# Two queue steps between the levels of a gated recurrence, and a weight request moved ahead of two row loads, in a fused decoder layer

## The chip, the cores and the metric

The kernel runs on 1 core of one Trainium2 chip, as one program. The metric is device time in microseconds of one execution. The kernel before took 1952.87 us (median of 3 runs, 1950.09 to 1953.01).

## The reference

One layer of a hybrid decoder for 1024 prompt tokens and 8x8 sample tokens, which share all weights. With D_MODEL 1024 and D_FF 2816, all in f32:

```python
x = x + 0.5 * rms_norm(swiglu(rms_norm(x, norm_ffn1_pre[l]), ffn1_w_gu[l], ffn1_w_down[l]), norm_ffn1_post[l])
h = rms_norm(x, norm_mix_pre[l])
z = h @ w_in[l] + b_in[l]
q, k, v, hq, hf, hi, hg = jnp.split(z, [...], axis=-1)
a, k_new, v_new = attend(q, k, v, attn_sinks[l])        # window of 128, 8 heads over 2 kv heads, a sink per head
a = rms_norm(a, attn_out_norm[l])
f = lb + (1.0 - lb) * jax.nn.sigmoid(hf)                # 4 heads of 128 keys and 128 values
o, S = hgrn2_chunked(silu(hq), 1.0 - f, jnp.log(f), hi, s0)
o = rms_norm(o, hg_out_norm[l]) * jax.nn.silu(hg)
mix = jnp.concatenate([a, o], axis=-1) @ w_out[l]
x = x + rms_norm(mix, norm_mix_post[l])
x = x + 0.5 * rms_norm(swiglu(rms_norm(x, norm_ffn2_pre[l]), ffn2_w_gu[l], ffn2_w_down[l]), norm_ffn2_post[l])
```

Within a chunk the recurrence needs, for query t and key s at or before it, the sum over key channels of q_t, k_s and the product of all gates f between s and t.

## The kernel before, in words

**Columns and precision.** The tokens stand as columns in three groups of 320 (256 prompt tokens and the 64 sample tokens), 384 and 384 (WIDTH). An f32 operand is split in a high and a low part of a faster format: `split` casts the high part on ScalarE (line 222) and subtracts it on VectorE for the low part (line 223). A product is then three matmuls, lines 245 to 247; the third is the one that takes the weights' low part. Weights come through `raw` tiles by SyncE's DMAs.

**The start.** `pre_first` makes the first two products of group 0 from data that it loads in an order of its own. Then it requests the high and low halves of the first unit's other weights (`wts.fill(1)`), loads the rows of x by tokens for the norm (line 635, three tiles: two of 128 rows, one of the 64 sample rows), squares and sums each on ScalarE (`squares`, line 642), and requests the second unit's up weights (`wts.fill(2)`). With the three sums come the root, three diagonal tiles (line 656) and a matmul that spreads the root over all partitions (line 661), copied by line 662. Gates multiply by it (line 698), go through Silu (line 699) and are multiplied by the up product (line 702).

**The feed-forward network of groups 1 and 2** is done by a scheme of seven products per pair of column halves, products 1, 6, 2, 5, 3, 7 and 4 of the down projection, one after another by `pair`. Each takes weights (lines 951 and 954, tiles `raw`, split into `w`) and stored activations (line 966: `ar<-fa`, a tile `ar` of 384 KB, split into a tile `h`). Of these requests one stands ahead in products 5, 3, 7 and 4 (`Ahead` with 1). A bank of four in `mm` is emptied by `put` (lines 979 to 995): an addition on VectorE, or a copy on ScalarE.

**The recurrence** of a group is `intra`, a generator. K (keys), Q (queries) and D (gate products) are kept for 384 columns. First the diagonal (tile `ld`), then levels h = 1, 2, 4, ..., 64: at each, small matmuls of 32x32 (line 1267, bank `lv`) or hxh (line 1307, banks `l32`, `l64`) join keys of the first half of each block of 2h with queries of the second half. VectorE takes the right cells over (line 1297) and multiplies the second halves of Q by gate products (line 1316), GpSimd the first halves of K (line 1318). The next level's matmuls need both. After each level stands a `yield`.

**What sets the order.** The attention and the recurrence of a group are put in two queues, "at" and "hg", by `ready` with a count of the steps of each generator. After each piece of a large product `tick` calls `pace`, which adds to each queue's account the steps left over the ticks left until the group is due (`DUE`: 132, 208, 256); when the two accounts hold 2, or one holds 1.5, both queues go one step on. So the recurrence of group 0 runs beside products 5 and 3 and those that follow, and the steps of "at" come at the same moments. Within that, the framework fixes each engine's instruction order when the program is built: each engine works down one list.

Of the kernel before, what the change touches and what calls it, by code (L numbers as in the profile page):

```python
# [27 lines left out]
NPB = [2, 3, 3]  # L28
# [16 lines left out]
def tile_step(ctx: ExitStack, tc: tile.TileContext, A: dict, O: dict):  # L45
# [10 lines left out]
    def uid(s):  # L56
        cnt[0] += 1
        return f"{s}_{cnt[0]}"
# [4 lines left out]
    def axbank(s="ax"):  # L63
        return ps.tile([P, 512], F32, tag="ax", bufs=4, name=uid(s))
# [5 lines left out]
    def big(dt=F32, shape=(P, 4, 384)):  # L70
        return pp.tile(list(shape), dt, tag="big", bufs=10, name=uid("big"))
# [197 lines left out]
    def rows_of(n, i):  # L269
        return min(P, WIDTH[n] - i * P)  # L270

    def new_h(n):
        return [[hslot(n), hslot(n)], [hslot(n), hslot(n)]]
# [271 lines left out]
    def pre_first(wgu, h, wts):  # L545
# [6 lines left out]
        def queued(eng):  # L552
            return tc.issue_after(last[eng]) if eng in last else nullcontext()

        def do(eng, make):
            with queued(eng):
                last[eng] = make().ins
# [71 lines left out]
        sm = small()  # L629
        V.memset(sm[:, 0], 1.0)  # L630
        rows = []
        for i in range(3):
            r = rows_of(0, i)
            t = big(F32, (P, D))
            nc.sync.dma_start(t[:r], A["x_prompt"][0, i * P:(i + 1) * P] if i < 2 else
                              A["x_sample"].rearrange("b t d -> (b t) d"))
            rows.append(t)

        def squares(i):
            r = rows_of(0, i)  # L640
            t = rows[i][:r]
            do("ACT", lambda: S.activation(t, t, AF.Square, scale=RMS, accum_out=sm[:r, 0, i:i + 1]))

        squares(0)
        squares(1)
        with queued("ACT"), queued("DVE"):
            wts.fill(2)
        last["ACT"], last["DVE"] = formed[1].ins, formed[0].ins
        squares(2)
        do("ACT", lambda: S.activation(junk[:, :P], ones, AF.Silu))  # L650
        do("DVE", lambda: V.tensor_scalar(ms0[:, 0:3], sm[:, 0, 0:3], EPS, None, op0=ALU.add))
        root(sm[:, 1, 0:3], ms0[:, 0:3])
# [390 lines left out]
    def mixing(tp, h):  # L1043
# [206 lines left out]
        def intra(n):  # L1250

            z, w, wp = Z[n], WIDTH[n], P * NPB[n]
            f, Q = z["f"][:, :, :w], z["hq"][:, :, :w]
            K = tp.tile([P, 4, 384], F32, tag="K", name=uid("K"))[:, :, :w]
            D = tp.tile([P, 1524], F32, tag="D", name=uid("D"))
            C = tp.tile([P, 3, 4, 32], F32, tag="cm", name=uid("cm"))
            parts = [(slice(0, P), slice(0, NPB[n]))] + ([(slice(0, NS), slice(2, 3))] if n == 0 else [])

            def span(h):
                return w if h <= 4 else wp  # L1260

            def blocks(s, x, y, h):
                b4 = axbank(s)[:, :384].rearrange("p (j a t) -> p j a t", j=3, a=4)
                for a in range(4):
                    for i in range(span(h) // 32):
                        j, cs, ps_ = i // 4, slice(32 * i, 32 * i + 32), slice(32 * (i % 4), 32 * (i % 4) + 32)
                        PE.matmul(b4[ps_, j, a], x[:, a, cs], y[:, a, cs], start=True, stop=True)  # L1267
                return b4

            def flat(t, rs, js):  # L1270
                return t[rs, js].rearrange("p j a t -> p (j a) t")

            S.activation(K, f, AF.Copy, bias=1.0, scale=-1.0)
            Ds, off, h = [f], 0, 1
            while h <= 64:
                nx = span(h) // (2 * h)
                Dv = Ds[-1][:, :, :2 * nx].rearrange("p a (x e) -> p a x e", e=2)
                Ds.append(D[:, off:off + 4 * nx].rearrange("p (a x) -> p a x", a=4))
                G.tensor_tensor(Ds[-1], Dv[:, :, :, 0], Dv[:, :, :, 1], op=ALU.mult)
                off += 4 * nx  # L1280
                h *= 2
            b4 = blocks("ld", K, Q, 1)
            for rs, js in parts:
                c = flat(C, rs, js)
                V.tensor_tensor(c, flat(b4, rs, js),
                                ident32[rs].unsqueeze(1).to_broadcast([c.shape[0], c.shape[1], 32]), op=ALU.mult)
            V.tensor_tensor(Q, Q, f, op=ALU.mult)
            yield
            At = z["f"]
            h = 1  # L1290
            while h <= 64:
                ws = span(h)
                if h <= 16:
                    b4 = blocks("lv", K, Q, h)
                    for rs, js in parts[:2 if h <= 4 else 1]:
                        c = flat(C, rs, js)
                        V.copy_predicated(c, lmask[h][rs].unsqueeze(1).to_broadcast([c.shape[0], c.shape[1], 32]),
                                          flat(b4, rs, js))
                else:
                    for j0 in range(0, NPB[n], 64 // h + 1):  # L1300
                        js = range(j0, min(NPB[n], j0 + 64 // h + 1))
                        b4 = axbank(f"l{h}")[:, :len(js) * 4 * h].rearrange("p (j a t) -> p j a t", j=len(js), a=4)
                        for j in js:
                            for a in range(4):
                                for c in range(0, P, 2 * h):
                                    k0 = j * P + c
                                    PE.matmul(b4[c:c + h, j - j0, a], K[:, a, k0:k0 + h], Q[:, a, k0 + h:k0 + 2 * h],
                                              start=True, stop=True)
                        Av = At[:, :, P * j0:P * j0 + P * len(js)].rearrange("p a (j t) -> p j a t", j=len(js))
                        for c in range(0, P, 2 * h):  # L1310
                            for j in range(len(js)):
                                S.copy(Av[c:c + h, j, :, c + h:c + 2 * h], b4[c:c + h, j])
                nx = ws // (2 * h)
                Qv, Kv = [t[:, :, :ws].rearrange("p a (x u) -> p a x u", u=2 * h) for t in (Q, K)]
                Dv = Ds.pop(0)[:, :, :2 * nx].rearrange("p a (x e) -> p a x e", e=2)
                V.tensor_tensor(Qv[:, :, :, h:], Qv[:, :, :, h:], Dv[:, :, :, 0:1].to_broadcast([P, 4, nx, h]),
                                op=ALU.mult)
                G.tensor_tensor(Kv[:, :, :, :h], Kv[:, :, :, :h], Dv[:, :, :, 1:2].to_broadcast([P, 4, nx, h]),
                                op=ALU.mult)
                if h == 1:  # L1320
                    G.memset(At[:, :, :w], 0.0)
                if h == 4 and n == 0:
                    z["Ds"] = Ds[0]
                if h == 16:
                    for i in range(4):
                        r, nj = slice(32 * i, 32 * i + 32), 3 if n == 0 and i < 2 else NPB[n]
                        Av = At[r, :, :384].rearrange("p a (j t) -> p j a t", j=3)
                        for j in range(nj):
                            G.tensor_copy(Av[:, j, :, r], C[r, j])
                h *= 2  # L1330
                yield
            z["K"], z["D"] = K, Ds[0]

        def finish_hgrn(n, bank, r, c0):
# [171 lines left out]
        def kv_out(n):  # L1506
            kx, vn = KX[n], VN[n]
            if n == 0:
                nc.sync.dma_start(O["ksT"], kx[:, P + 256:P + 256 + NS])
                for b in range(8):  # L1510
                    nc.sync.dma_start(O["vs"][0, b, 120:128].rearrange("j g d -> j (g d)"), vn[8 * b:8 * b + 8, 3])
            else:
                nc.sync.dma_start(O["kp"], kx[:, P + 256:P + 256 + P])
                nc.sync.dma_start(O["vp"], vn[:, 3])
            yield

        def ready(kind, n):
            if n not in MT:
                MT[n] = new_h(n)
            if kind == "at":  # L1520
                gens = [(attn_block(n, b), 9) for b in range(NPB[n])]
                if n == 0:
                    gens += [(sample_attn(), 11), (kv_out(0), 1)]
                if n == 2:
                    gens.append((kv_out(2), 1))
            else:
                gens = [(intra(n), 8)] + [(hgrn_block(n, b), 3) for b in range(NPB[n])]
                if n == 0:
                    gens.append((sample_hgrn(), 14))
                if n == 2:  # L1530
                    gens.append((state_out(), 1))
            queues[kind] += [[n, g, left] for g, left in gens]
# [50 lines left out]
    h = {}  # L1583
# [231 lines left out]
```

## Time and profile before

| | |
|---|---|
| Runs | 1952.87, 1953.01, 1950.09 us |
| The profiled execution | 1954.31 us |
| Its span, first to last instruction | 1952.6 us |
| TensorE matmuls busy | 1937.5 us (99%) |
| VectorE, ScalarE, GpSimd busy | 1349.6, 929.0, 211.1 us |
| Mean granted TensorE clock | 0.998 |
| Moved by DMA | 362.65 MB, 186 GB/s |

A row of a timeline reads: start in us from the start of the span, us, engine, line, operation, output tile <- input tiles, sizes, count; in brackets the idle time of the engine ahead of it and what ended it. PE is TensorE's matmuls, DVE VectorE, ACT ScalarE, POOL GpSimd, SP SyncE, which issues most DMAs. A row of a table of waits reads: engine, tile, line <- what it waited for: us in total, times, the longest. A row of a table of windows has, for each stretch: its length, the busy time of PE, of its weight loads, of DVE, ACT and POOL with their counts, the granted clock, the share of the DMA engines' time, and GB/s. A row of the chain of waits has: start, us, and the work or the DMA that the end hung on. The line numbers are those of the kernel before; in the kernel after they are 3 higher from the rest of `pre_first` on, and 5 higher behind `intra`.

### The profile page before, as it was taken

The page shows a single profiled execution, that of the slowest core. Times are in us where ns is not written, and L with a number is a line of the kernel's source. Part 1 is how long each engine was busy: PE and PEld are TensorE (multiplying, and loading weights), DVE is VectorE, ACT ScalarE, POOL GpSimd, SP SyncE. Part 2 cuts the span into 40 slices and gives each one's busy share as a digit, 9 for nine tenths or more (in the row PEclk, how much of TensorE's full clock was granted, in tenths as well). Part 3 has the DMA queues.
Part 4 walks back from the last instruction along what each step waited for, and adds up shares of the span by engine and source line. Part 5 has one row for each costly group of instructions (what it writes and reads, how often), then busy time and mean ns, then how long its engine had stood idle before and what let it go on. Part 6 is the DMA issues. An engine that isn't in the chain of part 4 may idle for free.

```text
span 1952.6 us, 34158 instructions
## 1 busy us (share of the span) xinstructions
PE 1937.5 (99%) x13451; PEld 1825.4 (93%) x13451; DVE 1349.6 (69%) x2188; ACT 929.0 (48%) x1637; POOL 211.1 (11%) x213
## 2 busy tenths in 40 slices
PE   9999999999999999999999999999999999999998
PEld 9999999999998987788899898999999999999887
DVE  5876667776558666875667765745987877655666
ACT  6633333444445544654345455745544444444453
POOL 0000000000004112111232431101000000000202
PEclk9999999999999999999999999999999999999999
DMA  9643345556677555675434333556555645577974
GB/s 322 209 143 129 144 162 186 179 183 208 236 236 228 163 146 163 213 228 153 120 101 141 115 112 117 190 166 206 174 204 187 217 177 186 206 237 232 308 260 141
DMA packets 162492, 362.65 MB, mean 186 GB/s; under 512 B 16524, under 2 KB 60236, under 8 KB 162316
## 3 DMA queue, kind: packets, MB, share of 16 engines
q1 hardware_dynamic: 161324, 358.65, 55.5%
q8 instruction: 105, 1.72, 0.4%
q10 hardware_dynamic: 1008, 1.84, 0.3%
q14 instruction: 55, 0.45, 0.1%
HBM read 283.78 MB, written 77.63 MB: 185 GB/s over the span
## 4 chain that ended last, share of the span: by engine, by line
PE 94%; DMA 2%; DVE 2%; ACT 1%; issue 1%; POOL 0%; SPq 0%; DVEq 0%; POOLq 0%; ACTq 0%
PE mm L245 28%; PE mm L247 28%; PE mm L246 28%; PE c L247 1%; PE c L245 1%; PE c L246 1%; DMA ar<-fa 1%; PE pv L1234 1%; PE sc L1193 1%; PE pT L1219 1%; PE lv L1267 0%; DMA raw<-in_ffn_w_gu_dram 0%; DMA x1N<-big 0%; PE av L1368 0%; DMA big<-in_x0T_dram 0%
## 5 line engine op out<-in xcount | busy, mean ns | idle before, releaser
L245 PE MATMUL mm<-h,wsph 128*128 128x320 f32 (+1 forms) x1280 | 409.5, 320 | 0.2 <-DVE sg L702 0.2
L247 PE MATMUL mm<-h,wspl 128*128 128x320 f32 (+1 forms) x1280 | 403.5, 317 | 1.2 <-DVE wspl L223 1.2
L246 PE MATMUL mm<-h,wsph 128*128 128x320 f32 (+1 forms) x1280 | 404.4, 316 | 0.0
L223 DVE TENSOR_TENSOR wspl<-raw,wsph 128x1024 fp32r<-128x1024 f32 x200 | 250.0, 1251 | 156.4 <-ACT wsph L222 156.0
L222 ACT CAST wsph<-raw 128x1024 fp32r<-128x1024 f32 x200 | 209.3, 1048 | 270.6 <-PE mm L246 205.4
L222 ACT CAST w<-raw 128x512 fp32r<-128x512 f32 (+1 forms) x226 | 169.3, 754 | 240.3 <-PE mm L246 119.8
L223 DVE TENSOR_TENSOR w<-raw,w 128x512 fp32r<-128x512 f32 (+1 forms) x226 | 196.6, 874 | 87.8 <-ACT w L222 87.3
L245 PEld LDWEIGHTS mm<-h,wsph 128*128 128x128 f32 x1280 | 240.4, 188 | 5.4 <-issue 3.2
L247 PEld LDWEIGHTS mm<-h,wspl 128*128 128x128 f32 x1280 | 239.9, 188 | 3.0 <-DVE wspl L223 1.7
L246 PEld LDWEIGHTS mm<-h,wsph 128*128 128x128 f32 x1280 | 240.5, 188 | 1.5 <-issue 0.7
L245 PE MATMUL mm<-h,w 128*128 128x384 f32 x704 | 235.6, 335 | 0.0
L246 PE MATMUL mm<-h,w 128*128 128x384 f32 x704 | 235.6, 335 | 0.0
L247 PE MATMUL mm<-h,w 128*128 128x384 f32 x704 | 230.5, 335 | 0.0
L245 PE MATMUL mm<-w,h 128*128 128x512 f32 x462 | 182.2, 398 | 1.9 <-DVE big L979 1.0
L246 PE MATMUL mm<-w,h 128*128 128x512 f32 x462 | 181.0, 392 | 0.0
L247 PE MATMUL mm<-w,h 128*128 128x512 f32 x462 | 178.9, 392 | 0.0
L216 POOL TENSOR_TENSOR sm<-sm,mhalf 128x3 f32<-128x3 f32 (+4 forms) x37 | 33.7, 913 | 1187.6 <-DVE sm L304 462.3
L245 PEld LDWEIGHTS mm<-h,w 128*128 128x128 f32 x704 | 132.2, 188 | 0.2 <-ACT big L793 0.2
L222 ACT CAST w<-t 128x512 fp32r<-128x512 f32 x176 | 107.3, 621 | 52.4 <-PE mm L247 46.9
L246 PEld LDWEIGHTS mm<-h,w 128*128 128x128 f32 x704 | 132.1, 188 | 0.0
L247 PEld LDWEIGHTS mm<-h,w 128*128 128x128 f32 x704 | 131.7, 188 | 0.0
L223 DVE TENSOR_TENSOR w<-t,w 128x512 fp32r<-128x512 f32 x176 | 119.0, 687 | 10.5 <-ACT w L222 10.3
(348 smaller groups left out, 3688.5 us busy)
## 6 DMA issues: line engine op xcount, KB each, us to landing
raw<-in_ffn_w_gu_dram SPq DMA_DIRECT2D x154, 512.0 KB
raw<-in_ffn_w_down_dram SPq DMA_DIRECT2D x74, 512.0 KB
raw<-in_w_in_dram SPq DMA_DIRECT2D x54, 512.0 KB
ar<-fa SPq DMA_DIRECT2D x70, 384.0 KB
big<-in_ffn_w_down_dram SPq DMA_DIRECT2D x88, 256.0 KB
fb<-big SPq DMA_DIRECT2D x44, 512.0 KB
raw<-fb SPq DMA_DIRECT2D x40, 512.0 KB
fa<-big SPq DMA_DIRECT2D x22, 768.0 KB
```

What stands on the lines that cost most here:

```text
L216: G.tensor_tensor(y, x, mhalf[:y.shape[0], :y.shape[1]], op=ALU.pow)
L222: formed[1] = S.copy(hi, src)
L223: return (lo_eng or V).tensor_tensor(lo, src, hi.bitcast(F32), op=ALU.subtract)
L245: PE.matmul(out, a[0], b[0], start=first, stop=False, skip_group_check=resume)
L246: PE.matmul(out, a[0], b[1], start=False, stop=False, skip_group_check=resume)
L247: r = latest[0] = PE.matmul(out, a[1], b[0], start=False, stop=last, skip_group_check=resume)
L1193: PE.matmul(banks[g][:, i * 256:i * 256 + wk], zq[64 * g:64 * g + 64, 2 * pr + i, b * P:(b + 1) * P], kx[64 * g:64 * g + 64, k0:k0 + wk], ...
L1219: PE.transpose(bank[:, (i * nk + kb) * P:(i * nk + kb + 1) * P], pt[g][:, i, kb * P:(kb + 1) * P], ident)
L1234: PE.matmul(ob[q0:q0 + 64, c:c + 64], pT[g][:, k1:k1 + 64], vn[:, vb, g * 64:g * 64 + 64], start=kb == 0, stop=kb == nk - 1)
```

## The change

There are two edits. `intra` gives way twice, not once, after each of the levels 1 to 32, and `ready` counts 14 steps for it, not 8. `pre_first` loads row tile 0, squares it, requests the second unit's up weights, and then loads and squares the row tiles 1 and 2.

```diff
-        for i in range(3):
+
+        def load_rows(i):
             r = rows_of(0, i)
             t = big(F32, (P, D))
             nc.sync.dma_start(t[:r], A["x_prompt"][0, i * P:(i + 1) * P] if i < 2 else
...
+        load_rows(0)
         squares(0)
-        squares(1)
         with queued("ACT"), queued("DVE"):
             wts.fill(2)
         last["ACT"], last["DVE"] = formed[1].ins, formed[0].ins
-        squares(2)
+        for i in (1, 2):
+            load_rows(i)
+            squares(i)
...
                 h *= 2
                 yield
+                if h <= 64:
+                    yield
...
-                gens = [(intra(n), 8)] + [(hgrn_block(n, b), 3) for b in range(NPB[n])]
+                gens = [(intra(n), 14)] + [(hgrn_block(n, b), 3) for b in range(NPB[n])]
```

The order on the engines changes at the start, and from the first level of group 0 until the last group's mixing is done. On ScalarE at the start, before (`raw_261`, `raw_272` and `raw_302` are the weights of the next units, `sg_332` and `sg_340` the first two gates):

```order
L642 ACTIVATE big_243,sm_237<-big_243 64x1024
L650 ACT_TABLE_LOAD
L650 ACTIVATE junk<-ones 128x128
L222 CAST wsph_263<-raw_261 128x1024
L699 ACTIVATE sg_332<-sg_332 128x320
L222 CAST wsph_274<-raw_272 128x1024
L699 ACTIVATE sg_340<-sg_340 128x320
L222 CAST wsph_304<-raw_302 128x1024
```

and after:

```order
L643 ACTIVATE big_251,sm_237<-big_251 64x1024
L653 ACT_TABLE_LOAD
L653 ACTIVATE junk<-ones 128x128
L222 CAST wsph_263<-raw_261 128x1024
L702 ACTIVATE sg_332<-sg_332 128x320
L702 ACTIVATE sg_340<-sg_340 128x320
L222 CAST wsph_274<-raw_272 128x1024
L222 CAST wsph_304<-raw_302 128x1024
```

The second gate's Silu has moved ahead of the cast of `raw_272`; its VectorE multiplication has moved ahead of that weight's low half in the same way.

On VectorE beside product 5 of the network, in the levels 4 and 8 of group 0, before (`h<-ar` are activation splits, the third, fourth and fifth of the product; `w<-raw` weight splits; `lm_87` is the mask of level 8; the last rows empty banks):

```order
L1316 TENSOR_TENSOR big_6608<-big_6608,D_6914 128x4x40x4
L223 TENSOR_TENSOR h_7611<-ar_7612,h_7611 128x2x384
L223 TENSOR_TENSOR w_7445<-raw_7442,w_7444 128x1024
L223 TENSOR_TENSOR h_7673<-ar_7674,h_7673 128x2x384
L1297 COPY_PREDICATED cm_6915<-lm_87,lv_7377 128x256
L1316 TENSOR_TENSOR big_6608<-big_6608,D_6914 128x4x16x8
L223 TENSOR_TENSOR w_7527<-raw_7524,w_7526 128x1024
L223 TENSOR_TENSOR h_7696<-ar_7697,h_7696 128x384
L979 TENSOR_TENSOR big_5843<-mm_7141,big_5843 128x512
```

and after (`lm_88` is the mask of level 4):

```order
L223 TENSOR_TENSOR h_7562<-ar_7563,h_7562 128x2x384
L223 TENSOR_TENSOR w_7416<-raw_7413,w_7415 128x1024
L223 TENSOR_TENSOR h_7591<-ar_7592,h_7591 128x2x384
L223 TENSOR_TENSOR w_7445<-raw_7442,w_7444 128x1024
L1162 TENSOR_TENSOR h_6452<-oT_7361,h_6450 128x4x128
L1300 COPY_PREDICATED cm_6915<-lm_88,lv_7368 128x256
L1300 COPY_PREDICATED cm_6915<-lm_88,lv_7368 64x128
L1319 TENSOR_TENSOR big_6608<-big_6608,D_6914 128x4x40x4
L223 TENSOR_TENSOR h_7614<-ar_7615,h_7614 128x384
L1407 COPY big_8323<-kx_6247 128x8x8
L982 TENSOR_TENSOR big_5843<-mm_7153,big_5843 128x512
```

Before, level 4's Q multiplication stands ahead of the third and fourth activation splits, and level 8's behind the fourth. After, level 4's stands behind the third and the fourth.

On TensorE the matmuls of large products between the levels' groups of small ones in group 0 are these:

| between | before | after |
|---|---|---|
| level 1 and 2 | 36 of 320 columns, 18 of 512 | 36 of 320, 36 of 512 |
| level 2 and 4 | 36 of 512 | 54 of 512 |
| level 4 and 8 | 28 | 21 (then the 4 `sc` products of an attention block) |
| level 8 and 16 | 20 | 78 (24 of them between the first 4 and the other 28 of level 8) |
| level 16 and 32 | 33 | 45 |

## The prediction

> **What bounds the kernel now.** I read the page first, then the table of what TensorE waited for, then the timeline at the two places that the change touches. From the page:
> ```profile
> PE 1937.5 (99%) x13451; PEld 1825.4 (93%) x13451; DVE 1349.6 (69%) x2188; ACT 929.0 (48%) x1637; POOL 211.1 (11%) x213
> ```
> TensorE is the bound: 1937.5 of 1952.6 us. The change removes no product, so all that it can bring or cost is TensorE's idle time, its clock, and the switches between kinds of products. Its waits above 0.2 (us in total, times, the longest):
> ```profile
> PE lv L1267 <- DVE big L1316: 2.1, 1, 2.1
> PE mm L247 <- DVE wspl L223: 1.2, 2, 0.7
> PE mm L561 <- DVE sm L630: 1.1, 1, 1.1
> PE mm L245 <- DVE big L979: 1.0, 1, 1.0
> PE tr L428 <- DVE h L433: 0.9, 1, 0.9
> PE mm L245 <- ACT h L222: 0.9, 1, 0.9
> PE pv L1234 <- DVE t L1222: 0.8, 1, 0.8
> ```
> Of all levels of the recurrence, in three column groups, one alone (first row) kept TensorE waiting for its Q. The two steps between levels aim at that row, the weights ahead of the rows of x at one of the two in the second row.
>
> **The weights ahead of the rows, step by step.** Timeline of the start: TensorE's stall and the two sides that feed it.
> ```profile
> 19.07 0.31 PE L246 MATMUL mm<-h,wsph 128*128 128x320 f32 x1
> 20.04 0.41 PE L247 MATMUL mm<-h,wspl 128*128 128x320 f32 x1 [0.66 <-DVE wspl L223]
> 18.76 1.23 DVE L223 TENSOR_TENSOR wspl<-raw,wsph 128x1024 fp32r<-128x1024 f32 x1 [4.16 <-ACT wsph L222]
> 15.33 1.06 ACT L642 ACTIVATE big<-big 128x1024 f32<-128x1024 f32 x1 [0.93 <-DMA big<-in_x_prompt_dram]
> 17.68 1.05 ACT L222 CAST wsph<-raw 128x1024 fp32r<-128x1024 f32 x1 [1.20 <-DMA raw<-in_ffn_w_gu_dram]
> ```
> Products of this shape start 0.15 us apart (rows below), here 0.97, so the stall takes 0.82. In the new queue order the weights come where row 1 came, so they land at about 15.33, their low half is out at 15.33+1.05+1.23, about 17.6, and TensorE asks at 19.2: this stall goes, −0.82, with 1.6 us to spare.
>
> What is late next is the low half two units on (raw_272 in the order):
> ```profile
> 24.81 0.47 ACT L699 ACTIVATE sg<-sg 128x320 f32<-128x320 f32 x1 [2.47 <-DVE sg L698]
> 25.38 1.05 ACT L222 CAST wsph<-raw 128x1024 fp32r<-128x1024 f32 x1
> 26.45 1.23 DVE L223 TENSOR_TENSOR wspl<-raw,wsph 128x1024 fp32r<-128x1024 f32 x1 [0.65 <-ACT wsph L222]
> 27.42 0.31 PE L245 MATMUL ax<-h,wsph 128*128 128x320 f32 x1
> 27.57 0.31 PE L246 MATMUL ax<-h,wsph 128*128 128x320 f32 x1
> 27.73 0.41 PE L247 MATMUL ax<-h,wspl 128*128 128x320 f32 x1
> ```
> It is ready at 26.45+1.23 = 27.68 and is taken at 27.73: no slack at all. TensorE, 0.82 earlier, would ask at 26.9. Does the low half come earlier too? Its cast stands behind both activations of line 699 now, not one: +0.37 (0.47 less the overlap). Ahead of that stand the three squares; the same bytes have landed by 17.7 in either order, but the last item is then the sample rows, 64 partitions, so the chain of the root, the spread and the first activation moves up by some 0.3. Together about 0: the stall moves from 19 to 27 us, and I put the net at −0.1. Bounds: −0.6 (chain up by 0.5 more than I think), +0.3 (the 0.37 without the 0.3). What follows to 51 us stands in nearly the same order and its second stall of 0.5 stays.
>
> **Two steps per level.** TensorE at the level wait, the clock after it, and a stretch with like idle time:
> ```profile
> 752.03 0.75 PE L1267 MATMUL lv<-big,K 128*32 128x32 f32 x64 [2.13 <-DVE big L1316]
> 755.31 0.80 PE L245 MATMUL mm<-w,h 128*128 128x512 f32 x1 [1.03 <-DVE big L979]
> 755.91 0.63 PE L246 MATMUL mm<-w,h 128*128 128x512 f32 x1
> 759.32 0.55 PE L245 MATMUL mm<-w,h 128*128 128x512 f32 x1
> 813.69 0.39 PE L246 MATMUL mm<-w,h 128*128 128x512 f32 x1
> 813.92 0.39 PE L247 MATMUL mm<-w,h 128*128 128x512 f32 x1
> ```
> ```profile
> 753.00:755.00 2.00, 1.29 (x3) 0.47 (x2) 0.93 (x3) 1.46 (x4) 1.01 (x1) 0.50 1.03 306
> 815.00:820.00 5.00, 3.15 (x17) 2.02 (x16) 5.00 (x8) 3.67 (x8) 3.26 (x2) 1.00 0.71 230
> ```
> (In the windows the granted clock is the third column from the end.) Idle 2.13 and 1.03. Then the clock stands at 0.50: from 755.91 to 759.32 the 8 products start 0.43 apart where 813.69 to 813.92 is 0.23, 1.6 us lost, and the five products on either side lose about 1.0 more. The place costs 2.13+1.03+2.6 = 5.8 us; that is the prize.
>
> Why Q was late, from the chain of waits and DVE's timeline:
> ```profile
> 743.91 0.76 PE L1267 MATMUL lv<-big,K 128*32 128x32 f32 x64
> 744.00 5.05 DMA ar<-fa
> 749.99 0.96 DVE L223 TENSOR_TENSOR h<-ar,h 128x768 fp32r<-128x768 f32 x1 [4.80 <-ACT h L222]
> 750.86 0.43 DVE L1297 COPY_PREDICATED cm<-lm,lv 128x256 f32<-128x256 uint8 x1
> 751.19 0.69 DVE L1316 TENSOR_TENSOR big<-big,D 128x512 f32<-128x512 f32 x1
> 750.98 2.48 DMA ar<-fa
> 754.57 1.29 DVE L979 TENSOR_TENSOR big<-mm,big 128x512 f32<-128x512 f32 x2
> 748.60 0.60 PE L1172 MATMUL oT<-ident,t 128*128 128x128 f32 x4
> 731.84 0.81 DVE L1316 TENSOR_TENSOR big<-big,D 128x640 f32<-128x640 f32 x1
> 758.07 0.68 DVE L1159 TENSOR_TENSOR h<-oT,h 128x512 fp32r<-128x512 f32 x1
> ```
> Level 8's products were done at 744.7; its Q multiplication could have followed. But DVE takes its queue in order, and the fourth ar split stood ahead of it, waiting for a cast behind a DMA of 5.05 us, which itself is issued only when the third split has freed its slot. Not the distance between levels was too short, but the wrong thing stood ahead. In the new order of DVE the fourth split (h_7591) stands ahead of level 4's copies and Q, with a weight split and the oT split between. So the same block is met one level earlier.
>
> Where TensorE will be: from level 1 to level 8 the order has 111 products of 512 columns instead of 82, besides 4 oT and 4 sc. 29×0.23+0.60+0.6 (sc like oT) = 7.9, so level 8 is reached at 743.9+7.9 = 751.8. Where Q will be, if the split is where it was: 750.86 + 1.14 (weight split, less overlap) + 0.60 (oT split) + 0.53 (copies) + 0.81 (Q at 640) = 753.9. Stall 2.1. Bounds: 0 to 3, since three such DMAs stand in the chain and they took between 2.48 and 5.36 us:
> ```profile
> 736.70 5.36 DMA ar<-fa
> ```
> After it, TensorE's next product takes a new bank, which waits for line 979's addition; that stands behind the fifth split, whose DMA (2.48) is issued when the fourth is done. The first addition began at 754.57 and TensorE went on at 755.31; with a small copy put ahead of it in the new order I take 755.5. TensorE idle from 754.1: 1.4 (bounds 0.5 to 2.1). Idle 3.5 in place of 3.16; if the clock then halves as before, 2.6 more: 6.1 in place of 5.8, **+0.3**.
>
> Beside it: level 8's products stand in two pieces, 4 and 28; a switch into small products costs 0.1 or so (start to start 0.28 in place of 0.15), so **+0.2**:
> ```profile
> 1136.28 0.31 PE L246 MATMUL mm<-h,wsph 128*128 128x320 f32 x1
> 1136.56 0.95 PE L1307 MATMUL l<-big,K 128*32 128x32 f32 x48
> ```
> The waits of lines 428, 245 (for a cast) and 1234, 0.9+0.9+0.8 = 2.6, are accidents of the old order. The new order draws afresh; I see two candidates of about 1 us (the pv products that follow level 16 closely, the transposes further on) and put **−0.6**, bounds −2.6 to +2. In groups 1 and 2 no level waited before, and wider spacing changes nothing there. GpSimd's K multiplications stay hidden: they follow the same products, and with more work up to the next level.
>
> Sum: −0.1+0.3+0.2−0.6 = −0.2, so 1954.1 against the profiled execution's 1954.31. That execution lay 1.4 above the median of the runs, 1952.87; I forecast 1952.6.
>
> **The rivals.**
> *Faster (24%):* the fourth split comes 2 us or more earlier, because the three DMAs take nearer 3 than 5 us at their new places. Then level 8 does not wait, the bank wait is some 0.8 and the clock stays up: 0.8−5.8 = −5.0, with −0.1+0.2−0.6 gives −5.5: 1947.4. For it: the spread 2.48 to 5.36. Against it: the two DMAs of this size (2.48 is half of it) took 5.05 and 5.36.
> *The clock stays up (12%):* waits as I forecast, but no half clock: −2.6 more, 1950.0. For it: in the window 815 to 820 TensorE was idle for 1.85 us and the clock stayed 1.00; 2.13+1.03 brought 0.50. The limit lies between, and my 2.1+1.4 is past it. [...]
> *Slower (19%):* the fourth split comes 1.5 us or more later than before, as its DMA meets the weight loads of a place where products run without a pause. Level 8 then waits 3.6, the bank 1.4, and the half clock lasts through two spells, 5.2: 10.2 in place of 5.8, +4.4, with the accidents unchanged +4.5: 1957.4. It decides from 1.5 us on; the DMA share of 1.03 in the window 753 to 755 speaks for it, that the chain of three starts no later speaks against.
> *The start keeps its 0.8 (3%):* if raw_272's chain moves up whole; 1952.0, the forecast otherwise.
>
> **How the numbers follow.** My forecast, the block one level earlier at about the same price, has 42%. 0.2% of this time, 3.9 us, is about what a measurement can tell from no change. Faster by more: 24 and a quarter of the clock case, 27%. Slower: 19 and 1 from the edge of my case, 20%. Within: 53%. The range takes in both signs, 1947.0 to 1957.5; the likeliest case's own is 1950.0 to 1955.0, by the bounds of bank and stall.
>
> **What would show it.** Right: no wait at 20 us but one of about 0.7 at 27 us for the low half (line 223); an lv wait for Q (line 1319) at 751 to 754, with level 8's first 4 products, then a wait for line 982; clock 0.50 there. Wrong: no lv wait in the list and a clock of 1.00 from 740 to 770 (faster), an lv wait above 3.5 us (slower), or a new wait above 2 us in groups 1 or 2, which I have not seen.

## The result and the profile after

The changed kernel takes 1960.66 us (median of 6 runs, 1959.40 to 1963.77), the kernel before 1950.53 (6 runs beside it, 1949.95 to 1953.01): ratio 1.0048, 95% interval 1.0037 to 1.0059. It is slower by 9 to 10 us, outside the forecast range (1947.0 to 1957.5). The profiled execution of after took 1961.22, span 1959.5, against 1954.31 and 1952.6: the two profiles lie 6.9 us apart, not 10, because the profiled execution of before took 3.8 us more than the median of those runs.

The page, and TensorE's table of waits above 0.2 us, after:

```profile
PE 1942.7 (99%) x13451; PEld 1828.4 (93%) x13451; DVE 1348.4 (69%) x2188; ACT 926.8 (47%) x1636; POOL 205.3 (10%) x213
```

```profile
PE pv L1237 <- DVE t L1225: 5.4, 2, 3.0
PE mm L561 <- DVE sm L630: 1.1, 1, 1.1
PE mm L245 <- ACT h L222: 0.8, 1, 0.8
PE ax L247 <- DVE wspl L223: 0.7, 1, 0.7
PE pT L1222 <- DVE sm L1345: 0.7, 1, 0.7
PE mm L247 <- DVE wspl L223: 0.5, 1, 0.5
PE mm L247 <- DVE h L223: 0.3, 1, 0.3
```

The level wait (lv for Q) is gone, and so is the wait for a bank behind it. In their place attention's pv products wait twice for VectorE's copy of pT, 3.0 and 2.4 us. Matmuls are busy for 5.2 us more, though the products are the same. The first of the two waits, in the timeline of TensorE, VectorE and ScalarE and in the chain of waits:

```profile
771.75 1.03 PE L1222 MATMUL pT<-ident,t 128*128 128x128 f32 x8
778.78 0.48 PE L1237 MATMUL pv<-vn,t 128*64 128x64 f32 x4 [3.03 <-DVE t L1225]
774.20 1.32 DVE L223 TENSOR_TENSOR h<-ar,h 128x768 fp32r<-128x768 f32 x1 [4.55 <-ACT h L222]
777.17 0.96 DVE L223 TENSOR_TENSOR h<-ar,h 128x768 fp32r<-128x768 f32 x1 [0.51 <-ACT h L222]
778.04 0.68 DVE L1225 COPY t<-pT 128x512 f32<-128x512 f32 x1
776.30 0.83 ACT L222 CAST h<-ar 128x768 fp32r<-128x768 f32 x1 [1.18 <-DMA ar<-fa]
```

```profile
770.09 6.13 DMA ar<-fa
```

The transposes pT were done at 772.8 and their copy takes 0.7. It ran at 778.0, because two activation splits stood ahead of it, the second of which waited for a DMA of 6.13 us. This is the mechanism that the prediction read off the level wait, with another victim. ScalarE's copy of the other half of pT stood behind the same load and ran at 777.99.

The second wait, from 1272.75 to 1275.11, is a blocked queue too, though no such load is near. VectorE's copy stands behind a weight split, and that waits for a cast, which ScalarE reaches only after a table load and four exponentials (1268.88 to 1272.26):

```profile
1268.88 1.28 ACT L1213 ACT_TABLE_LOAD   x1
1272.16 1.98 ACT L222 CAST wsph<-raw 128x1024 fp32r<-128x1024 f32 x2
1273.23 1.23 DVE L223 TENSOR_TENSOR wspl<-raw,wsph 128x1024 fp32r<-128x1024 f32 x1 [2.57 <-ACT wsph L222]
1274.37 0.68 DVE L1225 COPY t<-pT 128x512 f32<-128x512 f32 x1
```

Two stretches at half clock go with the two waits, from 777.82 to 784.65 and from 1276.17 to 1279.58 (the granted clock is the third column from the end):

```profile
777.00:779.00 2.00, 0.22 (x4) 0.22 (x6) 1.83 (x3) 1.56 (x3) 0.00 (x0) 0.70 0.56 131
781.00:783.00 2.00, 2.00 (x6) 1.52 (x6) 1.52 (x3) 1.62 (x3) 1.88 (x7) 0.50 0.41 122
783.00:785.00 2.00, 2.00 (x7) 1.59 (x6) 2.00 (x4) 1.22 (x4) 0.10 (x1) 0.59 0.71 196
1275.00:1277.00 2.00, 1.89 (x18) 1.13 (x20) 1.21 (x3) 1.36 (x2) 0.00 (x0) 0.79 0.74 213
1277.00:1279.00 2.00, 2.00 (x27) 1.88 (x28) 1.97 (x11) 0.00 (x0) 0.00 (x0) 0.50 0.77 158
1279.00:1281.00 2.00, 2.00 (x15) 2.00 (x14) 0.81 (x3) 1.68 (x2) 0.00 (x0) 0.86 0.63 239
```

At the start the stall has moved as forecast. TensorE, and the two engines that feed it:

```profile
28.41 0.42 PE L247 MATMUL ax<-h,wspl 128*128 128x320 f32 x1 [0.71 <-DVE wspl L223]
24.46 0.87 ACT L702 ACTIVATE sg<-sg 128x320 f32<-128x320 f32 x2 [2.31 <-DVE sg L701]
26.05 1.05 ACT L222 CAST wsph<-raw 128x1024 fp32r<-128x1024 f32 x1 [0.72 <-DMA raw<-in_ffn_w_gu_dram]
27.13 1.23 DVE L223 TENSOR_TENSOR wspl<-raw,wsph 128x1024 fp32r<-128x1024 f32 x1 [1.28 <-ACT wsph L222]
```

**Where the profiles differ.** I split each profile's span in four: TensorE's idle time between its first and last instruction (the gaps of its timeline, the ends left out), what is lost at a granted clock below 1 (busy time of each window of 1 us times 1 less the clock), the large products at their own pace, and the rest. The rest is the time of the small products and of the switches to and from them. Since the products are the same, its change is the span's change less the first two. Before: idle 7.1, clock 2.9. After: idle 9.0, clock 4.75. So of +6.9, +1.8 is idle time, +1.8 clock, and +3.2 rest, which no table of waits shows.

What a part of the rest is can be seen in the recurrence of the samples (`su`, a pair of products per head, one with its operands on partitions 0 to 31, the other on 32 to 63). Before, then after, both from the timeline:

```profile
891.62 1.13 PE L1499 MATMUL su<-t,m 32*128 32x512 f32 x4
910.17 1.13 PE L1499 MATMUL su<-t,m 32*128 32x512 f32 x4
```

```profile
899.62 1.12 PE L1504 MATMUL su<-t,m 32*128 32x512 f32 x2
901.04 1.12 PE L1504 MATMUL su<-t,m 32*128 32x512 f32 x2
```

The pair (4 records) takes 1.13 us side by side, its records starting in pairs 6 or 7 ns apart, and each half takes 1.12 where a large product has come between, its two records starting 533 ns apart: +1.05 for one torn pair.

The remainder can be sized from the same timelines, if each product is given the time from its start to the next product's start, without idle time and lost clock. Then the transposes pT and tr take 1.5 and 1.2 us more than before, `su` 1.05, and each of the other small kinds between 0.3 less and 0.5 more, while the large products (lines 245 to 247) take 2.5 less. The small products stand in 125 stretches between large ones, before in 147. So the new order switches less often, not more, and still the small products take longer.

### The profile page after: what moved, and what is told of

It is laid out like the page before. It is cut to its first block, busy times and chain, and to the rows that moved or that the text cites. A ratio compares the mean times of both kernels' runs of the same rounds, so it can differ in the third digit from the quotient of the medians.

```text
span 1959.5 us, 34136 instructions
## 1 busy us (share of the span) xinstructions
PE 1942.7 (99%) x13451; PEld 1828.4 (93%) x13451; DVE 1348.4 (69%) x2188; ACT 926.8 (47%) x1636; POOL 205.3 (10%) x213
## 4 chain that ended last, share of the span: by engine, by line
PE 92%; DMA 3%; DVE 2%; ACT 1%; issue 1%; SPq 0%; POOL 0%; DVEq 0%; POOLq 0%; ACTq 0%
PE mm L245 28%; PE mm L247 27%; PE mm L246 27%; PE c L245 1%; PE c L247 1%; PE c L246 1%; DMA ar<-fa 1%; PE pv L1237 1%; DMA xt<-in_x_prompt_dram 1%; PE sc L1196 1%; PE lv L1270 1%; PE pT L1222 1%; DMA big<-in_x_sample_dram 0%; DMA raw<-in_ffn_w_gu_dram 0%; DMA big<-in_x0T_dram 0%
## 5 line engine op out<-in xcount | busy, mean ns | idle before, releaser
L223 DVE TENSOR_TENSOR wspl<-raw,wsph 128x1024 fp32r<-128x1024 f32 x200 | 249.0, 1246 | 144.7 <-ACT wsph L222 144.4
```

What stands on the lines that cost most here:

```text
L223: return (lo_eng or V).tensor_tensor(lo, src, hi.bitcast(F32), op=ALU.subtract)
```

## The experiments

Ratios are to runs of the kernel before on the same chip, with 95% intervals. Theory A of the first batch: the two pv waits, with their half clock, make the loss. Rival B: the start does. Later ones: C, attention's steps are drawn together by the raised pace of the queues; D, the order's packing of small products. The changed kernel itself ran beside before at 1950.53; beside the experiments before stood at 1951.8 to 1952.5. So a difference between an experiment and the changed kernel is uncertain by 1 to 2 us, and where it matters the ratios decide.

### e1: the recurrence's part alone

The kernel before, with only these edits:

```diff
                 yield
+                if h <= 64:
+                    yield
...
-                gens = [(intra(n), 8)] + ...
+                gens = [(intra(n), 14)] + ...
```

> The second step between levels and the count of 14 alone; the start is that of the kernel before. Theory A (the two waits of the pv products for VectorE's copy of pT, at 775 and 1272 us of the changed kernel, 3.0 and 2.4 us, and the half clock behind each make the loss): the whole loss stays but for the start's 0.7 us, so 8 to 10 us slower than before, with both pv waits in the list. Rival B (the start's new order costs most): within 2 us of the kernel before.

Measured: 1960.06 us, ratio 1.0041 (1.0028 to 1.0054). To within the intervals the whole loss is here. Both pv waits are in the list (1.6 and 2.4), the first smaller than in the changed kernel, with a wait of 1.9 for a bank behind it. B falls.

### e2: the start's part alone

The changed kernel with the second `yield` taken out and the count back at 8.

> The weights ahead of rows 1 and 2 alone; the recurrence gives way once per level as before. By my prediction's step for the start the stall of 0.82 us moves from 19 to 27 us and nothing is won: 0 to +1.0 us against before, with a wait for the low half near 27 us, and the lv wait near 752 us still there. Rival B (the start's new order makes the loss): 8 us or more slower. A third view, that it wins its 0.8: 0.8 us faster.

Measured: 1952.09, ratio 0.9999 (0.9990 to 1.0008): nothing won, nothing lost. The lv wait that I expected to find again near 752 wasn't there, though the order in that place is that of before; only the wait for a bank behind it was:

```profile
753.00 0.50 PE L245 MATMUL mm<-w,h 128*128 128x512 f32 x1 [1.40 <-DVE big L982]
```

No half clock followed it. So the 5.8 us that this place cost in the profile of before are no fixed price: with the same order the place cost 1.4 here, and 1.41 in e11 and 1.46 in e6.

### e3: activations requested two ahead, changed kernel

```diff
-            AC[ms] = Ahead([...], 2 if inner else 1)
+            AC[ms] = Ahead([...], 2 if inner else 2)
```

> The changed kernel, with the stored activations of products 5, 3, 7 and 4 requested two ahead, not one. Theory A1 (the first pv wait comes from an activation split that stands in VectorE's queue and waits for its DMA): the pv wait at 775 us goes, with its half clock, 5 to 6 us; the one at 1272 us stays, since no such load is near it: 4 to 5 us slower than before. Rival C (the copy of pT is late because TensorE is asked for pv too soon after pT, whatever stands in the queue): the wait at 775 stays at 2 us or more and the time stays 8 to 10 us above before.

Measured: 1961.10, ratio 1.0044 (1.0031 to 1.0058); pv waits 5.5 us in total. The run didn't test what it was meant to: SyncE issued the two loads ahead of the wait at 768.35 and 769.89, in the changed kernel at 768.54 and 770.09, so they were not requested earlier.

### e4: the second step, the pace as before

```diff
-                gens = [(intra(n), 14)] + ...
+                gens = [(intra(n), 8)] + ...
```

> The changed kernel, but the queue still counts 8 steps for the recurrence although it gives way 14 times, so the pace of both queues, attention's steps too, is not raised in the first stretch. In the order pT and pv of the first attention block then stand 32 large products apart, not 9 behind level 16. Theory C (the raised count draws attention's steps together, and pv is asked for too soon): no pv wait at 775 us, 3 to 6 us faster than the changed kernel. Rival A1 (the blocked split alone): a wait of like size remains wherever the copy stands behind an activation split.

Measured: 1962.00, ratio 1.0048 (1.0036 to 1.0061). The pv wait at 775 is gone, as C has it, but the 3 to 6 us that I expected from it are not won. The waits are other ones (3.2 us for a Silu at 1285 the longest), and the rest is 7.9 us above before, with two torn pairs of `su`. The time is not carried by one wait.

### e5 and e6: group 0 alone, groups 1 and 2 alone

```diff
-                if h <= 64:
+                if n == 0 and h <= 64:
...
-                gens = [(intra(n), 14)] + ...
+                gens = [(intra(n), 14 if n == 0 else 8)] + ...
```

and for e6 `n > 0`, with 14 for those groups.

> The second step and the count of 14 in column group 0 alone; groups 1 and 2 as before; the start as in the changed kernel. The profile of the changed kernel has one pv wait in group 0 (775 us) and one in group 2 (1272 us). Theory A (the two pv waits with their half clock make most of the loss, each some 5 us): the first stays, the second goes: 3 to 5 us slower than before. Rival D (the loss lies in how small products are packed, over all groups): about half the loss, but with no tie to the waits.

> The second step and the count of 14 in groups 1 and 2 alone; group 0 as before; the start as in the changed kernel. Theory A: the wait near 775 goes and the lv wait near 752 (or its neighbour, the wait for a bank) is back; a pv wait near 1270 may stay, since the crowding there comes from these groups: 2 to 5 us slower than before. With e5 the two losses should add up to that of the changed kernel, 8 to 10 us.

Measured: e5 1966.22, ratio 1.0072 (1.0057 to 1.0087); e6 1956.47, ratio 1.0027 (1.0017 to 1.0037). The parts come to 14 us (3 to 5 expected) and 4 us, the whole to 8 to 10: they don't add up, and theory A doesn't hold as I put it. In e5 the first pv wait stays (3.1) and, in a stretch whose steps were not doubled, two other pv waits stand at 1246 and 1249 (2.26, 1.23). What group 0 does moves what follows.

### e7: one more attention step between pT and pv

```diff
                     pT.append(t)
                 yield
+                yield
...
-                gens = [(attn_block(n, b), 9) ...
+                gens = [(attn_block(n, b), 11) ...
```

> The changed kernel with one more step of the attention queue between pT and pv (count 11, not 9). In the order pv then stands 54 large products behind pT in group 0's block, where it was 9, and 24 to 26 in the last blocks. Theory C (pv is asked for too soon after pT): both pv waits go with their half clock, and the time falls by 5 us or more against the changed kernel, to 1952 to 1956. Rival D (packing and lumps at the end): the waits go, but the time stays above 1957.

Measured: 1958.96, ratio 1.0035 (1.0023 to 1.0047). Both pv waits and all half clock are gone, and yet only 2 us are won. The rest is 5.3 us above before; among other things two groups of `sc` are torn (2.0). This is what D said, but not packing alone: a new wait of 2.6 us, of attention's transposes `oT` for VectorE, stands at 1150.

### e8: each queue by its own account

```diff
-        while sum(owed.values()) >= 2.0 or max(owed.values()) >= 1.5:
-            for k, q in queues.items():
+        for k, q in queues.items():
+            while owed[k] >= 1.0:
                 owed[k] -= 1.0
```

> The changed kernel, but each queue goes a step on when its own account holds 1, so that the recurrence's six more steps no longer draw attention's steps along. In the order, pT to pv is 30 large products in the first full block (9 in the changed kernel, 30 before). Theory C' (the coupling of the two queues makes the loss): 5 us or more faster than the changed kernel. If attention's steps are not the matter: within 2 us of the changed kernel.

Measured: 1957.75, ratio 1.0026 (1.0016 to 1.0037), 3 to 4 us better than the changed kernel, between the two forecasts. Idle time is 3.8 us, 3.3 less than before, and still the kernel is slower than before: the rest is 8.3 us up. The scores of an attention block, in the timeline of before and then of e8:

```profile
1162.04 1.13 PE L1193 MATMUL sc<-kx,big 64*128 64x256 f32 x8
```

```profile
1115.30 1.13 PE L1196 MATMUL sc<-kx,big 64*128 64x256 f32 x4
1116.36 0.42 PE L245 MATMUL mm<-h,wsph 128*128 128x320 f32 x1
...
1118.31 1.13 PE L1196 MATMUL sc<-kx,big 64*128 64x256 f32 x4
```

A product has two records here. Four products take 1.13 us together, their records starting in pairs 6 or 7 ns apart (in before, from 1162.04 on); torn, two products take 1.13 as well. Two such groups and two of `su` make 4.2 of the 8.3; of the other half 1.9 lies in the large products, and in the small ones 0.8 (`tr`) is the most.

### e9 and e10: no loads of stored activations

Products 5, 3, 7 and 4 get zeros from GpSimd; the loads are left out, in the changed kernel (e9) and in the kernel before (e10).

```diff
-                nc.sync.dma_start(raw[:, :n], FA[:, k0:k0 + n, SLOT[m]])
+                if inner:
+                    nc.sync.dma_start(raw[:, :n], FA[:, k0:k0 + n, SLOT[m]])
+                else:
+                    G.memset(raw[:, :n], 0.0)
```

> The changed kernel, but products 5, 3, 7 and 4 don't load their stored activations: GpSimd fills the tiles with zeros instead, and the splits stay. Theory A1 (the first pv wait comes from the copies of pT standing in their queues behind an activation split that waits for a DMA of 6 us): the wait near 775 us shrinks from 3.0 to under 0.5, and with its half clock 5 to 6 us go; the wait at 1272 stays, since no such load is near. Rival C (pv is asked for too soon after pT, 9 products): the wait near 775 stays above 1.5 us.

> The kernel before with the same loads left out and zeros in their place. My prediction read the lv wait of 2.1 us at 752 as VectorE's queue held by an activation split that waits for its DMA. By that the lv wait, the wait for a bank behind it and the half clock go: 3 to 6 us faster than before, and no lv wait in the list. If the wait comes from the levels standing too close together, it stays at 1 to 2 us.

Measured: e9 1955.62, ratio 1.0020 (1.0011 to 1.0030), 5 us below the changed kernel; e10 1947.01, ratio 0.9977 (0.9968 to 0.9987), 4.8 below before. In e9 VectorE copies pT as soon as it is there, and pv doesn't wait:

```profile
771.21 1.03 PE L1225 MATMUL pT<-ident,t 128*128 128x128 f32 x8
775.14 0.45 PE L1240 MATMUL pv<-vn,t 128*64 128x64 f32 x8
771.85 0.69 DVE L1228 COPY t<-pT 128x512 f32<-128x512 f32 x1 [1.56 <-PE pT L1225]
```

Pv follows pT as closely as in the changed kernel (9 large products), so C falls for this wait: the split that waits for its load makes it. GpSimd's fills and the missing DMA traffic come with the edit, but the row shows the copy free to start as soon as pT is done. In e10 no wait for Q is left. The wait at 1272 stays in e9 (2.4), and so does a rest of +4.3.

### e11: the scores' loops swapped, kernel before

```diff
-                for i in range(2):
-                    for g in range(2):
+                for g in range(2):
+                    for i in range(2):
                         PE.matmul(banks[g][:, i * 256:i * 256 + wk],
```

> The kernel before with the two loops around the score products swapped, so that two products of the same half of the array's rows follow each other, not one of each half. The traces have such a group of four at 1.08 us, and a pair of it that the order has torn apart at 1.07, as if products of different halves ran at the same time. Theory D (pairs of small products that stand side by side run together, and a torn pair costs its whole time again): 1.5 to 1.6 us for a group of four, 14 groups, 6 to 8 us slower than before. If the array does one at a time: no change.

Measured: 1950.17, ratio 0.9989 (0.9980 to 0.9998). I was wrong on what tears a group: two products on partitions 0 to 63 followed by two on 64 to 127 take as long (1.14 us) as the four in turn (1.13, before).

```profile
764.88 1.14 PE L1193 MATMUL sc<-kx,big 64*128 64x256 f32 x8
```

So in both orders that I tried four products take 1.13 to 1.14 us with nothing else between; with a large product in the middle two of them alone took 1.13 (e8).

### e12: the raised pace alone

The changed kernel without the second `yield`; the count of 14 stays.

> The changed kernel without the second step in the recurrence, but with the queue still counting 14, so that only the pace of both queues is raised. With the e4 run (the second step, the count of 8) it splits the change in two. Theory C (the raised pace crowds attention's steps): 4 to 9 us slower than before with waits at pv or pT. Rival E (the recurrence's spread alone makes the loss): within 2 us of the kernel before.

Measured: 1959.58, ratio 1.0039 (1.0024 to 1.0054). Waits for five different things of 1.3 to 1.8 us, pv among them, and a rest of +4.0. With e4, either half of the recurrence's edit alone costs about as much as both.

### e13 and e16: four rows of activations in a load, kernel before; e14: the same, changed kernel

The slot of `ar` was half empty. Every second group finds its data loaded:

```diff
...
-                    raw = pp.tile([P, 2, 384], F32, tag="h384", bufs=8, name=uid("ar"))
-                nc.sync.dma_start(raw[:, :n], FA[:, k0:k0 + n, SLOT[m]])
+                    if k0 % 4 == 0:
+                        held[0] = pp.tile([P, 4, 384], F32, tag="h384", bufs=8, name=uid("ar"))
+                        nk = min(4, NK - k0)
+                        nc.sync.dma_start(held[0][:, :nk], FA[:, k0:k0 + nk, SLOT[m]])
+                    raw = held[0][:, k0 % 4:k0 % 4 + 2]
```

and in e16 also `Ahead([...], 2)`.

> The kernel before, with the stored activations of products 5, 3, 7 and 4 loaded four rows at a time, not two, into the same slot (it was half empty), so that every other split finds its data there already. By the reading that an activation split waiting for its DMA holds VectorE's queue (e10 won 4.8 us with no such loads at all): the wait near 752 shrinks or goes and 2 to 5 us are won against before. If the longer loads come late by as much as fewer of them save: within 1 us.

> As e13, and requested two groups ahead. If the slots allow the earlier request, a little faster than e13 (0 to 1 us); if they are full anyway, the same.

> The changed kernel with the same loads of four rows. The pv wait near 775 goes or falls under 1 us, with its half clock: 3 to 6 us faster than the changed kernel, and still 3 us or more slower than e13, since the wait near 1272 and the packing stay.

Measured: e13 1956.62, ratio 1.0018 (1.0010 to 1.0027), slower; e16 1948.53, ratio 0.9981 (0.9972 to 0.9990), which beats both kernels; e14 1957.59, ratio 1.0028 (1.0019 to 1.0037), 3 us below the changed kernel. In e13 the lv wait shrank to 0.15, but the 2 to 5 us that I expected are not won. Two waits for an activation's cast stand further on, 4.1 us together, the longer of them (2.8) behind a load of 6.72 us. Requested two groups ahead (e16), no wait for an activation's cast above 0.2 us is left (the lv wait is 0.5), idle time falls from 7.1 to 3.7, no half clock is left, and the rest stays within 0.5 of before. That is 8 us faster than e13, where I had expected 0 to 1. In e14 the pv wait at 775 is 1.49 in place of 3.03, and the other stays; it is 1 us slower than e13, not 3 or more.

### e15: the extra attention step in group 2 alone

As e7, with `if n == 2` at the second `yield` and 11 steps for that group.

> The changed kernel with one more attention step between pT and pv in group 2 alone. If the wait at 1272 comes from pv being asked for 4 products behind pT, it goes, 2.4 us and up to 1.7 of half clock; what else changes there is a new draw of the order. If it comes from ScalarE's chain of exponentials and table loads that stands ahead of the copies, a wait of 1 us or more remains in that stretch.

Measured: 1961.72, ratio 1.0044 (1.0030 to 1.0057). The wait at 1272 is gone, the one at 775 stays (3.1), and in the stretch from 1235 to 1251 stand four of 0.68 to 0.79. So the wait does hang on the distance between pT and pv: VectorE's copy runs at 1271.52, and pv is asked for only at 1274.15. The time is not won.

### What the runs say together

Change of the profile against before, in us, in the parts defined above (idle, clock, rest), with the span's:

| | idle | clock | rest | span |
|---|---|---|---|---|
| order of the mixing as before: e2 | -1.4 | -1.2 | +0.2 | -2.4 |
| e10 | -5.0 | -2.9 | +0.5 | -7.4 |
| e11 | -1.5 | -2.9 | +0.2 | -4.2 |
| e16 | -3.5 | -2.9 | +0.5 | -5.9 |
| e13 | +1.6 | -2.9 | +2.1 | +0.8 |
| order dealt anew: after | +1.8 | +1.8 | +3.2 | +6.9 |
| e1 | +3.4 | -1.3 | +3.6 | +5.7 |
| e3 | +1.5 | +3.5 | +2.3 | +7.3 |
| e4 | +1.0 | -1.2 | +7.9 | +7.7 |
| e5 | +5.0 | +1.7 | +4.3 | +10.9 |
| e6 | +0.9 | -2.9 | +3.6 | +1.5 |
| e7 | +2.9 | -2.9 | +5.3 | +5.3 |
| e8 | -3.3 | -1.2 | +8.3 | +3.8 |
| e9 | -1.7 | -1.3 | +4.3 | +1.3 |
| e12 | +2.4 | +0.2 | +4.0 | +6.6 |
| e14 | +0.8 | -1.2 | +4.7 | +4.3 |
| e15 | +3.3 | +0.5 | +5.2 | +9.0 |

The parts are of one profiled execution each, against the one of before. The rest is what sets the two blocks apart: 0.2 to 0.5 where attention and recurrence stand as before (2.1 in e13, whose order differs further on), 2.3 to 8.3 where they were dealt anew. Idle time and clock go both ways. How much one order's parts vary from execution to execution, these single profiles don't tell.

## Why the prediction was wrong, point by point

**The start: right, with some luck.** The stall moved from 19 to 27 us (0.71 there, about 0.7 forecast), and e2 puts the worth of the edit at zero, give or take 2 us, which is too wide to tell my bounds apart. One link differs: the two Silus did stand ahead of the cast (24.46, done at 25.33), but then the cast waited 0.72 more for its load and began at 26.05. I had no such wait in the sum.

**The level wait: wrong.** I had the fourth activation split where it was (749.99), a stall of 2.1 at level 8 and 1.4 at the bank. After, from VectorE's and TensorE's timelines:

```profile
746.57 0.96 DVE L223 TENSOR_TENSOR h<-ar,h 128x768 fp32r<-128x768 f32 x1 [2.95 <-ACT h L222]
750.94 0.81 DVE L1319 TENSOR_TENSOR big<-big,D 128x640 f32<-128x640 f32 x1
752.88 0.27 PE L1270 MATMUL lv<-big,K 128*32 128x32 f32 x8
```

The split came 3.4 us earlier, Q was ready at 751.75, and TensorE got there at 752.88, a microsecond later than I reckoned. That is what the faster rival said of this place. The link that failed here is "if the split is where it was". Its three loads took, in the chain of after:

```profile
731.20 3.99 DMA ar<-fa
737.12 3.30 DMA ar<-fa
742.35 3.27 DMA ar<-fa
```

In the profile of before the second and third took 5.36 and 5.05. It wasn't the new order that hastened them: with the old order in this place the same split began at 747.17 in e2, 747.50 in e6 and 747.58 in e11, so 749.99 was the exception. In e2:

```profile
747.17 0.96 DVE L223 TENSOR_TENSOR h<-ar,h 128x768 fp32r<-128x768 f32 x1 [3.04 <-ACT h L222]
```

**The prize: mis-sized.** I took 5.8 us from the profiled execution as what the place costs. In e2, e6 and e11, with the same order there, it cost 1.4 to 1.5. So most of what the change took away there the kernel paid in one of four profiles. The base was too high for the same reason: I took the profiled execution as 1.4 above the median, and beside the six runs it is 3.8.

**The accidents: the failed step.** I put the waits of the new order at -0.6 with bounds -2.6 and +2, and the pv products that follow level 16 closely were one of two candidates, at about 1 us. That wait measured 3.03, and the one at 1272, which I hadn't seen, 2.36. With 0.81, 0.32 and 0.68 beside them the accidents make 7.2 in place of 2.6: +4.6. The half clock behind them, 4.75, I had tied to the level wait alone. The prediction had named a new wait above 2 us in groups 1 or 2 as a sign against itself, and the one at 1272 is that. I had found the blocked queue and priced it for the one instruction that the change aims at; attention's copies stand in the same queue.

**Switches: mis-sized.** I had +0.2, for one torn level; the rest measured +3.2. The torn level itself came out as forecast (tile `lv`, +0.15 over the run). But I counted switches, which became fewer (125 stretches, not 147), and not what stands together: one torn `su` pair alone is 1.05.

**The sum by terms,** forecast and measured between the two profiles: the place +0.3 and −5.8 (its idle time 3.2 and 2.6 of its half clock are gone); accidents −0.6 and +4.6; half clock behind them 0 and +4.75; small products +0.2 and +3.2. The measured terms make +6.75 of the profiles' +6.9. The further 3 us to the medians' 10 are what the profile of before lay further above its median than that of after (3.8 and 0.6).

**The rivals.** Slower had 20% in all, 19 of them by a late fourth split. The sign came true, the mechanism did not: the split was early. The case "the clock stays up" had a limit between 1.85 us and 2.13+1.03 us of idle time; no such limit shows in the runs (last section), and in the profile of before half clock began at 752.81, with the 2.13 alone behind it. Shown by the runs: the loss is in the recurrence's part (e1, e2), its first wait is the split that waits for its load (e9), and re-dealing the order costs small-product time that the waits don't show (e4, e7, e8). Not settled: why pT and tr take longer in the new order, how much of the rest comes back without the torn pairs, and what the wait at 1272 costs by itself, since e15 took it away and four smaller ones came.

## What to carry to other kernels

Where one engine is 99% busy and small work is dealt between large by a planner, a change of the planner's pace is a new deal of everything behind it: price the whole list of waits that can be met, not the one that the change aims at, and look in the order for pairs of small products torn apart (1.05 us for one of `su` here). A wait in one profile is one draw (the place at 752 cost 5.8 us in one profile, 1.4 to 1.5 in three); other executions of the same order tell whether it is a cost. When a queue that is worked off in order holds an instruction that waits for a DMA, cure the load (e16: 1948.53 us against 1951.92), since a shift of the victims only changes who is behind it (pv's 3.03 us at 775 in the place of lv's 2.13 at 752).

## What the runs showed of the hardware

In these traces the length of a gap alone does not tell whether half clock followed. The same wait of 2.36 us at 1273 was followed by 3.4 us at half clock in the changed kernel (1276.17 to 1279.58; lost clock 1.7 by the windows above) and by none in e1:

```profile
1275.71 0.45 PE L1234 MATMUL pv<-vn,t 128*64 128x64 f32 x8 [2.36 <-DVE t L1222]
1275.00:1277.00 2.00, 1.28 (x16) 1.00 (x16) 1.79 (x3) 1.95 (x3) 0.00 (x0) 1.00 0.41 80
1277.00:1279.00 2.00, 2.00 (x36) 1.77 (x33) 1.74 (x9) 0.41 (x1) 0.00 (x0) 1.00 0.75 229
```

Gaps of 2.59 (e7, at 1150) and 2.83 (e13, at 827) were followed by none either, but one of 1.43 in e8 was:

```profile
810.70 0.55 PE L428 MATMUL tr<-ident,big 128*128 128x128 f32 x3 [1.43 <-DVE h L433]
813.00:815.00 2.00, 2.00 (x8) 1.63 (x7) 2.00 (x3) 0.88 (x2) 0.00 (x0) 0.50 0.04 16
```

And in e15 a spell of 3.4 us began at 901.3 though TensorE had not stood idle in the 70 us before it. What stands ahead of it is a torn `su` pair, 1.12 us each:

```profile
898.26 1.12 PE L1506 MATMUL su<-t,m 32*128 32x512 f32 x2
899.69 1.12 PE L1506 MATMUL su<-t,m 32*128 32x512 f32 x2
901.00:903.00 2.00, 2.00 (x8) 2.00 (x8) 1.84 (x5) 1.04 (x1) 0.00 (x0) 0.57 0.45 47
```

The torn pair of the changed kernel (899.62 and 901.04) was followed by none: the granted clock is 1.00 in every window from 896 to 915.

The spells were 3.4 us long here and 6.8 with the waits of 2.13 (before, 752.81 to 759.64) and 3.03 (after, 777.82 to 784.65), and 3.4 with one of 3.1 in e15 (778.4 to 781.8). Gaps of 1.43, 2.13 and 2.36 us were followed by half clock, gaps of 2.36, 2.59 and 2.83 by none; what decided it, no run here shows.

With nothing between them four products of `sc` took 1.13 us, in the swapped order (e11) 1.14; torn by large products (e8), two of them took 1.13. So in these runs half of a torn group took as long as the whole group together, as did half of a torn `su` pair (1.12 against 1.13).
